# Where the v requests stand in GpSimd's queue: each v behind the k of its unit, two stores held back at the end, half a row slot as first transfer

## The chip, the cores and the metric

One core of one Trainium2 chip. The metric is the device time of the whole kernel in microseconds (us). Every kernel is run several times. "Span" is the time from the first to the last instruction of the one run that was profiled. It lies 1 to 2 us below the device time of that run. An engine "lands" when its part of a transfer has arrived; each transfer is shared by all 16 DMA engines, and the first and the last of them can land some microseconds apart.

## The reference

Local attention in windows of 64 rows, fp32 in and out:

```python
B, S, D, W = 4, 4096, 1536, 64
q_w, k_w, v_w = (x.reshape(B, S // W, W, D) for x in (q, k, v))
logits = np.einsum('bnwd,bnud->bnwu', q_w, k_w) * D ** -0.5
attn = softmax(logits)                       # over u, the 64 keys of the window
out = np.einsum('bnwu,bnud->bnwd', attn, v_w).reshape(B, S, D)
```

Every element of q, k and v is read once and every element of the output is written once: 302 MB and 101 MB.

## The kernel before

The 16384 rows are worked in N = 32 units of 512 rows. A unit has three loads (q, k, v: 3 MB of fp32, which land as 1.5 MB of fp16) and one store (3 MB of fp32). GpSimd issues all of them, except the first load (raw q of unit 0) and the second half of the last store, which SyncE issues. GpSimd also hands each landed tile over to the buffer that TensorE reads: it waits for the landing, copies (2.75 us), and requests the next load into the buffer that is free again. So the order of GpSimd's program is the order of the requests, and all of them stand in one queue, q0.

```python
def load(name, u, dst, s):
    r = R if name == "v" else SLOTS          # v in pieces of 2 rows, q and k of 4
    nc.gpsimd.dma_start(out=slots(dst, 0, SLOTS, r), in_=rows(src, u * UR, SLOTS, r)).then_inc(s, 16)

def hand_over(src, dst, d, u, m, g):         # wait for landing and for a free target, copy, tell TensorE
    gp.wait_ge(d, 16 * u); gp.wait_ge(m, copies[0] // 3 + 1)
    gp.tensor_copy(out=dst[...], in_=src[...]).then_inc(c_l, 1)
    ...
# --- start: raw q of unit 0, three transfers by SyncE; the identity waits for the first of them
for sl, s in ((slice(0, 1), d_r0), (slice(1, 2), d_r1), (slice(2, SLOTS), d_r2)):
    nc.sync.dma_start(out=outs[0][:, sl, :], in_=raw[:, sl, :]).then_inc(s, 16)
...
for u in range(1, NV + 1):                   # NV = 2 buffers for v
    load("v", u, vls[u % NV], d_v[u % NV])
# --- the loop
for u in range(1, N):
    hand_over(ql, q16, d_q, u, m_q, g_q)
    if u + 1 < N: load("q", u + 1, ql, d_q)
    hand_over(kl, k16, d_k, u, m_k, g_k)
    if u + 1 < N: load("k", u + 1, kl, d_k)
    for what in {N - 3: "", N - 2: "-v"}.get(u, "s"):
        if what == "v": load("v", N - 1, vls[(N - 1) % NV], d_v[(N - 1) % NV])
        else:
            gp.wait_ge(m_q, u + 1)
            store(u - 2 if what == "-" else u - 1)
    if u == N - 2: store(u - 1)
    hand_over(vls[u % NV], v16, ...)
    if u + NV < N - 1: load("v", u + NV, vls[u % NV], d_v[u % NV])
# --- the end: two half stores of the last unit, one by GpSimd, one by SyncE; then gp.drain(), waits, clearing
```

The softmax here doesn't subtract the row's maximum and nothing guards it: scores larger than these inputs give would overflow.

## Time and profile before

| what | value | where |
|---|---|---|
| time | 946.71 us, 946.34 to 946.71 | median and range of 3 runs |
| span of the profiled run | 946.4 us (this run took 948.15 us, more than the three above) | page |
| DMA engines busy by q0 | 100.0% of 16 engines | page, queues |
| busiest compute engine | PE, 69% | page, engines |

A copy on GpSimd whose idle time was ended by a DMA marks the landing of its tile on the last of the 16 DMA engines. In a row of GpSimd's timeline stand start, duration, engine, line, operation and tiles, and in brackets the idle time just before with what ended it. The prediction shows the lines and reads them.

### The profile page before, as it was taken

Reading aid. Unit: us, or ns where it says so; the run is one execution under the profiler, and the core shown is the slowest. Engines: PE = TensorE matmul, PEld = TensorE weight load, DVE = VectorE, ACT = ScalarE, POOL = GpSimd, SP = SyncE. Lnnn points to the kernel's source line nnn. Section 1 sums busy time; section 2 is a strip of 40 time slices with the busy share of each in tenths; the row PEclk is TensorE's granted clock in tenths of the full one; section 3 lists DMA queues with packets and bytes.
Section 4 is the critical chain, followed back from the end, with each engine's and each line's share of the span. In section 5 each row is a group of like instructions: output and inputs, shape, how many; then the busy total and the mean of one; then the engine's idle time right before and its main releaser. Section 6 shows DMA issues by size and latency. Waiting matters only on the chain. (4 is left out here: it accounts for less than half of the span.)

```text
span 946.4 us, 11421 instructions
## 1 busy us (share of the span) xinstructions
PE 651.0 (69%) x4096; PEld 419.8 (44%) x3456; DVE 279.7 (30%) x453; ACT 332.8 (35%) x642; POOL 341.5 (36%) x229
## 2 busy tenths in 40 slices
PE   2776866768667676667777667866768666777682
PEld 2544543445534345434554344543435533445450
DVE  1333223332233231333313323223322233232331
ACT  1433323333334342333423334323333234343252
POOL 4323343233442334423344323343233442333520
PEclk9989777897878887798878789878898879797897
DMA  9999999999999999999999999999999999999997
GB/s 250 216 229 270 283 281 282 242 257 283 281 280 258 243 282 282 278 270 236 278 282 280 279 238 265 282 280 282 249 251 283 283 281 264 238 279 283 197 315 321
DMA packets 26940, 253.35 MB, mean 268 GB/s; under 512 B 2096, under 2 KB 2096, under 8 KB 10544
## 3 DMA queue, kind: packets, MB, share of 16 engines
q0 software_dynamic: 26352, 248.52, 100.0%
q1 hardware_dynamic: 576, 4.72, 1.3%
q14 instruction: 10, 0.08, 0.0%
q8 instruction: 2, 0.03, 0.0%
HBM read 301.99 MB, written 100.66 MB: 425 GB/s over the span
## 5 line engine op out<-in xcount | busy, mean ns | idle before, releaser
L147 PE MATMUL tp<-ident,q 128*128 128x128 f32 x768 | 165.0, 384 | 185.6 <-PEq L213 172.7
L147 PEld LDWEIGHTS tp<-ident,q 128*128 128x128 f32 x768 | 131.2, 200 | 239.4 <-issue 236.8
L292 POOL COPY q<-ql 128x3072 f32<-128x3072 f32 x31 | 85.0, 2743 | 395.7 <-DMA ql<-in_q_dram 395.5
L159 PE MATMUL lt<-xq,xk 128*128 128x256 f16 x1536 | 210.2, 288 | 0.0
L147 PE MATMUL tp<-ident,k 128*128 128x128 f32 x768 | 136.3, 317 | 67.3 <-PEq L213 54.5
L159 PEld LDWEIGHTS lt<-xq,xk 128*128 128x128 f16 x1536 | 156.8, 102 | 30.4
L222 ACT COPY xq<-tp 128x512 f32<-128x512 f32 x96 | 60.2, 627 | 291.2 <-ACTq L213 291.2
L147 PEld LDWEIGHTS tp<-ident,k 128*128 128x128 f32 x768 | 105.1, 163 | 86.3 <-issue 83.9
L222 DVE COPY xq<-tp 128x512 f32<-128x512 f32 x96 | 66.4, 692 | 254.7 <-DVEq L213 254.7
L222 ACT COPY xk<-tp 128x512 f32<-128x512 f32 x96 | 59.8, 623 | 228.6 <-ACTq L213 228.6
L222 DVE COPY xk<-tp 128x512 f32<-128x512 f32 x96 | 66.5, 693 | 198.6 <-DVEq L213 198.6
L292 POOL COPY k<-kl 128x3072 f32<-128x3072 f32 x31 | 85.3, 2751 | 110.5 <-DMA kl<-in_k_dram 110.5
L264 ACT ACTIVATE et<-lt,zeros 32x128 f16<-32x128 f32 x256 | 92.0, 359 | 39.4 <-ACTq L213 36.1
L188 PEld LDWEIGHTS <-et 128*128 128x128 f16 x384 | 30.2, 97 | 152.7 <-issue 116.7
L115 PE MATMUL o<-v,et 128*128 128x512 f16 x384 | 93.3, 379 | 0.0
L251 DVE TENSOR_SCALAR out<-o,rs 128x512 f32<-128x512 f32 x128 | 90.2, 747 | 7.7
L292 POOL COPY v<-vl 128x3072 f32<-128x3072 f32 x31 | 85.5, 2758 | 10.4 <-DMA vl<-in_v_dram 10.4
L115 PE MATMUL tp<-v,et 128*128 128x512 f16 x256 | 75.8, 377 | 0.0
L241 DVE RECIPROCAL rs<-sp 128x2 f32<-128x2 f32 x64 | 10.6, 166 | 162.6 <-DVEq L213 162.4
L275 ACT ACTIVATE out<-tp,rs 128x512 f32<-128x512 f32 x64 | 44.0, 688 | 37.2 <-ACTq L213 31.3
L251 DVE TENSOR_SCALAR out<-tp,rs 128x512 f32<-128x512 f32 x64 | 48.1, 751 | 26.2 <-DVEq L213 26.2
L115 PE MATMUL lt<-v,et 128*128 128x512 f16 x128 | 48.3, 377 | 0.0
(22 smaller groups left out, 201.2 us busy)
## 6 DMA issues: line engine op xcount, KB each, us to landing
out_dram<-out POOLq DMA_DIRECT2D x31, 3072.0 KB, 32.5
ql<-in_q_dram POOLq DMA_DIRECT2D x31, 1536.0 KB, 25.8
kl<-in_k_dram POOLq DMA_DIRECT2D x31, 1536.0 KB, 25.8
vl<-in_v_dram POOLq DMA_DIRECT2D x31, 1536.0 KB, 35.7
out<-in_q_dram SPq DMA_DIRECT2D x2, 768.0 KB, 6.5
out<-in_q_dram SPq DMA_DIRECT2D x1, 1536.0 KB, 11.2
k<-in_k_dram POOLq DMA_DIRECT2D x1, 1536.0 KB, 12.2
v<-in_v_dram POOLq DMA_DIRECT2D x1, 1536.0 KB, 18.8
```

The costliest lines, as they stand in the source:

```text
L115: return nc.tensor.add_instruction(mybir.InstMatmult(name=nc.get_next_instruction_name(), engine=PE, ins=[low(rhs), low(w)], outs=[low(o)] ...
L147: ins = nc.tensor.transpose(tps[g % 2][:, r, j, :], pairs[:, c * P : (c + 1) * P], ident[:, :])
L159: ins = nc.tensor.matmul(lts[h][:, r, :, :], lhsT=halves(xk, c)[:, r, h, :, w], rhs=halves(xq, c)[:, :, h, :, w], start=(c == 0 and w == 0 ...
L188: ld = nc.tensor.ldweights(w)
L222: copy(out=dst, in_=tps[g % 2][:, :, :, :]).then_inc(f_c[g % 4], 1)
L241: ve.reciprocal(out=rs[:, n : n + R], in_=sp[:, n : n + R]).then_inc(n_d, 1)
L251: ins = ve.tensor_scalar_mul(scaled(u, n, j), bank(n, j), scalar1=rs[:, n : n + 1])
L264: ins = sc.activation(ets[h][s, :, :, s], lts[h][s, :, :, s], EXP, bias=zeros[s, 0:1], scale=scale)
L275: ins = sc.activation(scaled(u, n, j), bank(n, j), COPY, bias=0.0, scale=rs[:, n : n + 1])
L292: gp.tensor_copy(out=dst[:, :, :].bitcast(FP32), in_=src[:, :, :].bitcast(FP32)).then_inc(c_l, 1)
```

## The change

Its intent: request v(u+1) right behind k(u+1), instead of v(u+2) after the copy of v(u). At the end the last loads are then all queued before the two stores that were held back, so the queue does not run dry between them. At the start the first transfer is half as large, so that the identity, and the first request behind it, come sooner.

```diff
@@ start: the first row slot as two halves
-        for sl, s in ((slice(0, 1), d_r0), (slice(1, 2), d_r1), (slice(2, SLOTS), d_r2)):
-            nc.sync.dma_start(out=outs[0][:, sl, :], in_=raw[:, sl, :]).then_inc(s, 16)
+        for lo, hi, c0, c1, s in (
+            (0, 1, 0, D // 2, d_r0), (0, 1, D // 2, D, d_r1), (1, 2, 0, D, d_r2), (2, SLOTS, 0, D, d_r3)
+        ):
+            nc.sync.dma_start(out=outs[0][:, lo:hi, c0:c1], in_=raw[:, lo:hi, c0:c1]).then_inc(s, 16)
   [...]
         load("k", 1, kl, d_k)
-        for u in range(1, NV + 1):
-            load("v", u, vls[u % NV], d_v[u % NV])
+        load("v", 1, vls[1], d_v[1])
@@ loop
             if u + 1 < N:
                 load("k", u + 1, kl, d_k)
-
-            for what in {N - 3: "", N - 2: "-v"}.get(u, "s"):
-                if what == "v":
-                    load("v", N - 1, vls[(N - 1) % NV], d_v[(N - 1) % NV])
-                else:
-                    gp.wait_ge(m_q, u + 1)
-                    store(u - 2 if what == "-" else u - 1)
-            if u == N - 2:
+                load("v", u + 1, vls[(u + 1) % NV], d_v[(u + 1) % NV])
+
+            if u != N - 3:
+                gp.wait_ge(m_q, u + 1)
+                if u == N - 2:
+                    store(u - 2)
                 store(u - 1)
             hand_over(vls[u % NV], v16, d_v[u % NV], (u + u % NV) // NV, m_v, g_v)
-            if u + NV < N - 1:
-                load("v", u + NV, vls[u % NV], d_v[u % NV])
```

More of the change, by code (lines that the diff above doesn't have):

```diff
@@ L74 @@
     sp = ps("sp", [P, 4])
-    d_r0, d_r1, d_r2, d_q, d_k, d_k0, d_v0 = (
-        sem(n) for n in ("d_r0", "d_r1", "d_r2", "d_q", "d_k", "d_k0", "d_v0")
+    d_r0, d_r1, d_r2, d_r3, d_q, d_k, d_k0, d_v0 = (
+        sem(n) for n in ("d_r0", "d_r1", "d_r2", "d_r3", "d_q", "d_k", "d_k0", "d_v0")
     )
@@ L301 @@
         raw = rows(qf, 0, SLOTS, SLOTS).rearrange("p h (r d) -> p (h r) d", d=D)
-        for sl, s in ((slice(0, 1), d_r0), (slice(1, 2), d_r1), (slice(2, SLOTS), d_r2)):
-            nc.sync.dma_start(out=outs[0][:, sl, :], in_=raw[:, sl, :]).then_inc(s, 16)
+        for lo, hi, c0, c1, s in (
+            (0, 1, 0, D // 2, d_r0), (0, 1, D // 2, D, d_r1), (1, 2, 0, D, d_r2), (2, SLOTS, 0, D, d_r3)
+        ):
+            nc.sync.dma_start(
+                out=outs[0][:, lo:hi, c0:c1], in_=raw[:, lo:hi, c0:c1]
+            ).then_inc(s, 16)
         nc.vector.memset(ident[:, :], 0.0).then_inc(i_d, 1)
@@ L314 @@
         for i in range(SLOTS):
-            nc.gpsimd.wait_ge((d_r0, d_r1, d_r2, d_r2)[i], 16)
+            nc.gpsimd.wait_ge((d_r1, d_r2, d_r3, d_r3)[i], 16)
             nc.gpsimd.tensor_copy(out=q16[:, i, :], in_=outs[0][:, i, :]).then_inc(c_q, 1)
```

## The prediction

> **What bounds the kernel now.** I read the page from the top: engine shares, slices, DMA queues, traffic, the ended chain, then the DMA issues. After that came the stage table, and last GpSimd's own timeline, because GpSimd issues nearly every transfer.
>
> ```profile
> PE 651.0 (69%) x4096; PEld 419.8 (44%) x3456; DVE 279.7 (30%) x453; ACT 332.8 (35%) x642; POOL 341.5 (36%) x229
> ...
> DMA  9999999999999999999999999999999999999997
> GB/s 250 216 229 270 283 281 282 242 257 283 281 280 258 243 282 282 278 270 236 278 282 280 279 238 265 282 280 282 249 251 283 283 281 264 238 279 283 197 315 321
> ...
> q0 software_dynamic: 26352, 248.52, 100.0%
> ...
> HBM read 301.99 MB, written 100.66 MB: 425 GB/s over the span
> ```
>
> No compute engine is above 69%, while the DMA row is at 9 in every slice but the last, and GpSimd's queue q0 alone fills 100% of the 16 engines. So the transfers bound it. The GB/s row counts landed bytes: a load reads fp32 and lands fp16, so it counts half of what it reads. Counted by the larger side, load and store cost alike, and all of it, 402.65 MB, runs at 425 GB/s. The chain of waits is useless here: its pieces cover under 1 us around 929 us, because what ends the span is a store, and the chain does not follow that.
>
> ```profile
> 840.00:856.00 16.00, 8.73 (x60) 3.49 (x39) 4.57 (x8) 7.21 (x15) 2.76 (x2) 0.87 1.05 221
> 868.00:884.00 16.00, 9.62 (x68) 4.22 (x46) 5.26 (x9) 7.21 (x15) 2.20 (x1) 0.96 1.04 219
> 884.00:888.00 4.00, 2.98 (x13) 2.60 (x14) 0.69 (x1) 0.62 (x1) 1.08 (x2) 0.50 0.94 178
> 888.00:892.00 4.00, 2.29 (x13) 1.53 (x11) 1.39 (x2) 1.26 (x2) 2.75 (x1) 0.82 1.06 224
> 892.00:904.00 12.00, 10.53 (x86) 7.64 (x78) 2.65 (x5) 5.28 (x12) 8.15 (x6) 1.00 0.96 188
> ...
> 924.00:932.00 8.00, 5.42 (x32) 0.80 (x9) 4.57 (x8) 3.72 (x6) 0.55 (x1) 1.00 1.02 433
> ```
>
> The last two columns are DMA share and GB/s landed. Loads alone land 219 to 221 (twice that is read), stores alone 433. In two stretches of loads, 884 to 888 and 892 to 904 us, the share falls below 1 and the rate to 178 and 188. These are the only weak stretches between the start and the final drain.
>
> ```profile
> 823.47 2.74 POOL L292 COPY q<-ql 128x3072 f32<-128x3072 f32 x1 [13.16 <-DMA ql<-in_q_dram]
> ...
> 852.64 2.74 POOL L292 COPY q<-ql 128x3072 f32<-128x3072 f32 x1 [13.16 <-DMA ql<-in_q_dram]
> ...
> 863.86 2.76 POOL L292 COPY v<-vl 128x3072 f32<-128x3072 f32 x1
> 881.80 2.75 POOL L292 COPY q<-ql 128x3072 f32<-128x3072 f32 x1 [15.18 <-DMA ql<-in_q_dram]
> 885.13 0.53 POOL L108 DMA_DIRECT2D ql<-in_q_dram  x1 [0.58 <-POOL q L292]
> 889.07 2.75 POOL L292 COPY k<-kl 128x3072 f32<-128x3072 f32 x1 [3.41 <-DMA kl<-in_k_dram]
> 892.41 0.53 POOL L108 DMA_DIRECT2D kl<-in_k_dram  x1 [0.58 <-POOL k L292]
> ...
> 906.36 2.75 POOL L292 COPY k<-kl 128x3072 f32<-128x3072 f32 x1 [5.57 <-DMA kl<-in_k_dram]
> ...
> 929.57 0.55 POOL L382 DMA_DIRECT2D out_dram<-out  x1 [5.89 <-ACT out L275]
> ```
>
> A copy that waits for a landing marks it. Two q copies lie 29.17 us apart: one unit is three loads and a store, so 29.17 / 4 = 7.29 us per transfer. From 889.07 (k of unit 30 landed) to 906.36 (k of unit 31) only two transfers land, yet it takes 17.29 us where 2 x 7.29 = 14.58 are due: 2.7 us lost. The reason is in the issue times. In that iteration the store and the v of the last unit are deferred, so when q of unit 31 is requested at 885.13 only the rest of k 30 is queued (landed by 889.07), and k 31, requested at 892.41, has only q 31 ahead of it. The queue is nearly dry twice.
>
> **What the Trainium skill says.** "DMA: Bandwidth & Descriptors", section "Issuing engines are not separate DMA queues": transfers started by different engines run on the same 16 DMA engines and interleave, so the issuer saves only issue time. The trace agrees: loads and stores add up to one 425 GB/s. The same page, "Specifications", gives a fabric ceiling of 435 GB/s for a core; stores alone reach 433 here, so there is no headroom to find in a reordering, only idle time. The same page, "Anatomy of one DMA — SWDGE (gpsimd) path", puts a fixed cost of about 2 us on a transfer issued from GpSimd. That is hidden while others are queued; the 2.7 us above is where it shows.
>
> **The change part by part.**
>
> 1. v behind k. Before, GpSimd queues q(u+1), k(u+1), store(u-1), v(u+2); after, q(u+1), k(u+1), v(u+1), store(u-1). Same transfers, same sizes, and no instruction is added to any engine in the loop (229 on GpSimd are reordered; SyncE has 11 rows for 10). Per unit the bytes stay, so 29.17 us stay. When q lands there are still k, v and a store behind it, about 22 us of backlog. Gain 0.
>
> 2. The tail. Store 28 and store 29 are held until the v of unit 31 is requested. The requests now run k 30, v 30, q 31, k 31, v 31, store 28, 29, 30, 31. q 31 is requested 3.3 us after q 30 lands (881.80 to 885.13 above), with k 30 and v 30 behind it: 2 x 7.29 - 3.3 = 11 us of backlog. k 31 then has v 30 and q 31 ahead of it, the same 11 us. Neither can run dry, so the 2.7 us return. A second count: before, 12 transfers remain when q 29 lands at 852.6, so 852.6 + 12 x 7.29 = 940.1; the last store landed at 929.57 + 13.3 (page, issues) = 942.9, 2.8 us late. A third: against 220 GB/s the weak stretches lack (42 x 4 + 32 x 12) / 220 = 2.5 us. I take 2.7.
>
> 3. Does compute then become the end? After, q 29 lands one transfer earlier (its v no longer precedes it), at 845.3; k 31 at 845.3 + 8 x 7.29 = 903.6, v 31 at 910.9, stores 28, 29, 30 at 918.2, 925.5, 932.8. From a k copy to the first output was 14.4 us (889.07 to 903.50) and to the end of the last 19.6 us (889.07 to 908.69). Unit 31 writes the buffer that store 28 empties, so 903.6 + 14.4 = 918.0 meets 918.2: it may wait a microsecond, and be done near 924 or 925. The queue has work to 932.8. The last half stores join a busy queue with 8 us to spare, against 5 before (942.9 - 7.3 - 930.6). The end stays the DMA's.
>
> 4. The start. The first transfer is 384 KB instead of 768 KB, so the wait of 6.5 us before the identity, and with it the first k request at 7.51, comes earlier: half of 0.79 MB at 420 GB/s is 0.9 us, and more (1.5) if the cold first microsecond is shared. The engines are fed from 2 us on and in the 8 to 12 us windows their share is 1.01 and 1.06, so I find at most 0.5 us there; I count 0.2. Two extra issues are one more row on SyncE, 0.44 us (1.33 / 3), in parallel.
>
> Sum: 946.7 - 2.7 - 0.2 = 943.8 us.
>
> **The rivals.** (a) A hidden bound: v now lands only 7.3 us after its k, is copied by 10.1 us (with 2.75 us of copy), and the weighted product needs it 12.9 us after the k copy starts (889.07 to 902.00). It has 2.8 us of slack; if late DMA engines eat that, PE waits, but PE already idles 5.8 us per unit ahead of the q transposes (185.6 us on the page over 32 units), so the time stays at 943.8. (b) The start turns bad: the early k shares the engines with the rest of raw q, in packets that are larger, so raw q lands 3 to 5 us later and the first matmul moves from 16.4 to about 20. PE is late by that in unit 0, catches up within two units, and requests are queued deep by then; worth 0. (c) Nothing comes back, because the 2.7 us is lost for another reason, such as a slow DMA engine or GpSimd writing four requests in a row; then 946 to 947. Against it: the same copies and requests happen in every unit with no dip in the rate. (d) Three loads in a row or two stores in a row run slower than an alternation. Stores alone (433) and loads alone (2 x 220) are both at full rate, so no.
>
> **Range and chances.** The mechanism leaves a gain between 1 us (one of the two holes stays) and 4.5 us (tail, start, and a slow DMA engine lagging less). That gives 942.3 to 945.6. 2% is 19 us; nothing in the idle columns is that large, and the work is unchanged: within 2% at 0.985.
>
> **What would show it.** Right: the steady distance of q copies still 29.2 us; k 30 to k 31 with three transfers between (v 30, q 31, k 31) at about 3 x 7.29 = 21.9 us; load stretches near the end at 219 or more; last half stores issued near 925 and landing some 15 us later. Wrong: a new hole after the last loads, GpSimd waiting for v in the loop long enough to delay q requests, a unit longer than 29.3 us, or the last stores issued after 933, which would put compute at the end.

## The result, and the profile after

| | median | range | runs |
|---|---|---|---|
| before | 946.71 us | 946.34 to 947.0 | 4 |
| after | 950.02 us | 948.98 to 952.19 | 4 |

The ratio of after to before is 1.0038, with a 95% interval of 1.0017 to 1.0059. A ratio here is the mean time of one kernel's fast runs over that of the other's of the same rounds, so it is not quite the ratio of the medians. The class, within 2%, came as predicted, but the time did not: 3.3 us slower by the medians where 2.9 us faster was said, and outside the range of 942.3 to 945.6. The run of after that was profiled (948.98 us, span 947.2 us) was its fastest, so its trace shows less of the loss than the median has. The profiled run of before took 948.15 us, 1.4 us more than its median. The two traces therefore stand closer together than the two kernels do.

These are the lines of after's page that answer to those of before.

```profile
DMA  9999999999999999999999999999999999999997
GB/s 252 218 226 267 284 281 276 241 257 282 281 282 248 246 283 282 281 264 238 277 283 281 274 238 267 283 282 277 238 258 283 283 277 250 247 282 283 217 326 304
...
q0 software_dynamic: 26352, 248.52, 100.0%
...
HBM read 301.99 MB, written 100.66 MB: 425 GB/s over the span
```

The page looks as before. The engines count as busy, the same bytes move, and the rate of 425 GB/s is the same to three digits. A loss of 0.4% is not to be seen here, and a DMA engine that works longer on a packet than usual counts as busy all the same.

The table by stage of after, with the stretches of the end; the last two columns are DMA share and GB/s landed.

```profile
868.00:884.00 16.00, 9.01 (x48) 3.88 (x28) 5.54 (x10) 6.00 (x12) 3.30 (x2) 0.79 1.01 217
884.00:888.00 4.00, 1.49 (x12) 1.18 (x11) 1.10 (x2) 1.25 (x2) 2.81 (x2) 0.88 1.06 220
888.00:892.00 4.00, 3.87 (x19) 3.02 (x18) 1.38 (x2) 0.62 (x1) 2.66 (x5) 0.50 1.04 218
892.00:904.00 12.00, 11.25 (x82) 6.76 (x64) 3.03 (x5) 5.99 (x13) 5.42 (x2) 0.92 1.02 216
...
942.00:944.00 2.00, 0.00 (x0) 0.00 (x0) 0.00 (x0) 0.00 (x0) 0.00 (x0) 0.50 0.07 31
```

The two weak stretches of before (178 and 188 GB/s) are gone: all the last loads run at 216 to 220. In the last line, from 942 to 944 us, a share of 0.07 is left, where before has 0.01: a few DMA engines are late. The last four of the 16 landings of GpSimd's half store are at 942.09, 943.07, 943.52 and 943.69 us. In before a single one is late, at 942.87, and the next landed at 940.88.

GpSimd's timeline of after, one unit of the loop and the end.

```profile
818.86 2.75 POOL L292 COPY q<-ql 128x3072 f32<-128x3072 f32 x1 [11.82 <-DMA ql<-in_q_dram]
826.13 2.75 POOL L292 COPY k<-kl 128x3072 f32<-128x3072 f32 x1 [3.39 <-DMA kl<-in_k_dram]
829.48 0.54 POOL L108 DMA_DIRECT2D kl<-in_k_dram  x1 [0.60 <-POOL k L292]
830.01 0.71 POOL L108 DMA_DIRECT2D vl<-in_v_dram  x1
830.70 0.73 POOL L281 DMA_DIRECT2D out_dram<-out  x1
833.60 2.74 POOL L292 COPY v<-vl 128x3072 f32<-128x3072 f32 x1 [2.17 <-DMA vl<-in_v_dram]
848.15 2.75 POOL L292 COPY q<-ql 128x3072 f32<-128x3072 f32 x1 [11.81 <-DMA ql<-in_q_dram]
...
884.61 2.74 POOL L292 COPY k<-kl 128x3072 f32<-128x3072 f32 x1 [3.40 <-DMA kl<-in_k_dram]
...
906.54 2.75 POOL L292 COPY k<-kl 128x3072 f32<-128x3072 f32 x1 [4.53 <-DMA kl<-in_k_dram]
...
926.06 0.54 POOL L383 DMA_DIRECT2D out_dram<-out  x1 [8.98 <-ACT out L275]
```

Four things are to be seen. The q copies are 848.15 - 818.86 = 29.29 us apart, and over 23 units the mean is 29.31 us (before 29.23). Three requests stand back to back from 829.48 to 831.43, and this is while v is landing: its last engine is done at 833.60. Behind that v stands a store, so in these microseconds the engines pass from a load to a store. From k 30 to k 31 it takes 906.54 - 884.61 = 21.93 us, as predicted for three transfers. And the last half stores are requested at 926.06, long before the queue is empty, so compute is not the end.

**Two counts over the trace's packet records.** A transfer is split into packets. In the loop a load packet of q or k takes 926 ns (12288 bytes landed) and one of v 474 ns (6144 bytes); a store packet of 12288 bytes takes 460 ns. I counted between 200 and 840 us the load packets that took over 40 ns more than that, and the store packets that took 465 to 560 ns (leaving out 473 ns, a value that every kernel shows). The excess is given as the time of one engine per unit. The kernels named below before appear in the experiments; in those whose names begin with vq, v is requested right behind q.

```
                     load packets stretched   store packets stretched
                     count  engine-us/unit    count  engine-us/unit
before                  24   0.21               71   0.06
after                  166   1.31              236   0.23
whole_start            278   2.36              260   0.24
store_late              52   0.29              175   0.19
late_from_2              1   0.01              183   0.20
store_behind_q           3   0.01              172   0.21
v_behind_q              25   0.18                0   0.00
vq_control              18   0.14                0   0.00
vq_delayed              34   0.21                1   0.00
vq_delayed_9            87   0.77                5   0.01
```

In after the stretched load packets are nearly all of v (2.55 of the 2.56 us that the mean engine loses this way from 40 to 875 us; before loses 0.39). In the unit above there are 16 of them, and they begin between 828.2 and 831.7 us. Six of these had ended by 829.3, before the first request's record begins at 829.48. Over the loop 41 of after's 166 stretched load packets end before the first request of their unit begins, and 128 of 278 in whole_start. So nearness to the requests is seen, but a request that stretches only what is under way during it does not account for all of these packets.

**Where the span ends.** The two half stores of the last unit land last. I took the mean of their landings over the engines, the lag from there to the very last landing, and what follows until the end of the span.

| kernel | mean landing | lag of the last | to the end of the span | span |
|---|---|---|---|---|
| before | 940.59 | 2.28 (GpSimd's half) | 3.50 | 946.37 |
| after | 939.70 | 3.99 (GpSimd's) | 3.50 | 947.20 |
| before_filled_tail | 937.88 | 3.22 (SyncE's) | 1.34 | 942.44 |
| late_from_2 | 937.70 | 5.75 (GpSimd's) | 3.50 | 946.95 |
| store_behind_q | 938.01 | 5.98 (GpSimd's) | 3.63 | 947.61 |
| v_behind_q | 938.03 | 2.46 (SyncE's) | 1.34 | 941.83 |
| vq_last_k_first | 938.61 | 2.63 (SyncE's) | 3.04 | 944.28 |

So between these two traces after gained 0.9 us on the mean engine, but its last engine is 1.7 us further behind the mean than that of before. (The profiled run of before was a slow one, see above.) The last column but one has its own reason: the drain of GpSimd ends 2.26 us after the landing of GpSimd's own half in 18 of the 20 traces, and 1.2 us of clearing follow. Where GpSimd's half is the last by far, the span ends 3.50 us after it; where SyncE's is, 1.34 us after that one.

### The profile page after: what moved, and what is told of

It is laid out like the page before. It is cut to its first block, busy times and chain, and to the rows that moved or that the text cites. A ratio compares the mean times of both kernels' runs of the same rounds, so it can differ in the third digit from the quotient of the medians.

```text
span 947.2 us, 11422 instructions
## 1 busy us (share of the span) xinstructions
PE 650.3 (69%) x4096; PEld 418.6 (44%) x3456; DVE 279.6 (30%) x453; ACT 332.3 (35%) x642; POOL 340.9 (36%) x229
## 5 line engine op out<-in xcount | busy, mean ns | idle before, releaser
L147 PE MATMUL tp<-ident,q 128*128 128x128 f32 x768 | 162.3, 379 | 190.0 <-PEq L213 175.2
L147 PEld LDWEIGHTS tp<-ident,q 128*128 128x128 f32 x768 | 129.1, 197 | 243.3 <-issue 241.3
L159 PE MATMUL lt<-xq,xk 128*128 128x256 f16 x1536 | 212.4, 290 | 0.0
L292 POOL COPY v<-vl 128x3072 f32<-128x3072 f32 x31 | 85.1, 2744 | 68.1 <-DMA vl<-in_v_dram 68.1
## 6 DMA issues: line engine op xcount, KB each, us to landing
out<-in_q_dram SPq DMA_DIRECT2D x1, 1536.0 KB, 13.3
out_dram<-out POOLq DMA_DIRECT2D x1, 1536.0 KB, 17.6
```

The source lines that it names most:

```text
L147: ins = nc.tensor.transpose(tps[g % 2][:, r, j, :], pairs[:, c * P : (c + 1) * P], ident[:, :])
L159: ins = nc.tensor.matmul(lts[h][:, r, :, :], lhsT=halves(xk, c)[:, r, h, :, w], rhs=halves(xq, c)[:, :, h, :, w], start=(c == 0 and w == 0 ...
L292: gp.tensor_copy(out=dst[:, :, :].bitcast(FP32), in_=src[:, :, :].bitcast(FP32)).then_inc(c_l, 1)
```

## The experiments

The theory after the result, here called the request theory: the requests k, v and store of one unit, in one run on GpSimd, fall into the microseconds in which the engines pass from v to a store, and this stretches the packets under way; the loop gets longer and eats the gain of the tail. The rivals: the new start costs it; the tail gains nothing; the landing of v just behind k makes GpSimd wait, which delays requests; or the order of the transfers itself, three loads in a row, is slow, whenever they are requested. Runs stand beside runs of before on the same chip: its medians were 947.12, 947.09, 947.05, 947.04 and 947.32 us in the five calls.

### First call

**half_start_only**: before with the new start alone.

The main line of the diff, cut:

```diff
+ (0, 1, 0, D // 2, d_r0), (0, 1, D // 2, D, d_r1), (1, 2, 0, D, d_r2), (2, SLOTS, 0, D, d_r3)
```

> The kernel before with only the half row slot first. Theory S (the start made the result worse: the early k and the last rows of raw q share the engines, one engine begins late and stays late): about 948 to 949 us, later engines' lag visible in k landings from the first unit on. Theory T (each unit loses time where the v load gives way to the store while requests are made): the start is worth nothing or up to 0.5 us, so 946.2 to 947.0 us.

Measured: 946.54 us (945.75 to 946.97), ratio 0.9993 (0.998 to 1.0006). The start does no harm, so the rival of the start falls. Its predicted gain of 0.2 us is inside what these runs cannot resolve.

**whole_start**: after with the start of before, so the rest of the change alone (the diff above, reversed).

> The changed kernel with the start of the kernel before. Theory S: the loss goes, 943.5 to 945 us. Theory T: the loss stays, 949 to 951 us, and single runs differ by 2 to 3 us as they do for the changed kernel.

Measured: 951.16 us (949.37 to 952.27), ratio 1.0038 (1.0025 to 1.0051). The loss does not sit in the start. It is the kernel with the most stretched load packets of all, 2.36 engine-us per unit, and its units take 29.41 us.

**late_requests**: after, but GpSimd hands v over before it requests k, v and store, which puts these three requests about 7 us later, behind the pass from v to the store.

```diff
             hand_over(kl, k16, d_k, u, m_k, g_k)
+            late = u < N - 3
+            if late:
+                hand_over(vls[u % NV], v16, d_v[u % NV], (u + u % NV) // NV, m_v, g_v)
             if u + 1 < N:
                 load("k", u + 1, kl, d_k)
   [...]
-            hand_over(vls[u % NV], v16, ...)
+            if not late: hand_over(vls[u % NV], v16, ...)
```

> The changed kernel, but in all units up to the last three the requests for k, v and the store are made after the copy of v, some 7 us later, when the engines are already in the store; the order of transfers in the queue is unchanged. Theory T1 (GpSimd writing three requests while v is loaded stalls the load): the stall goes, q copies 29.17 us apart, 944 to 945.5 us. Theory T2 (the switch of the engines from v load to store costs, whoever is issuing): nothing changes, 949 to 951 us and the v packets are still stretched.

Measured: 950.34 us (949.8 to 950.85), ratio 1.0032 (1.0019 to 1.0045). No gain, but the run does not speak against the request theory: the stretched load packets between 200 and 840 us are gone altogether (none), and the edit made a hole of its own near 54 us, where k of unit 2 was requested too late (1.25 us of the mean engine).

**before_filled_tail**: before with only its tail changed, so that v of the last unit is requested one iteration earlier and the stores are held as in after.

```diff
-            for what in {N - 3: "", N - 2: "-v"}.get(u, "s"): ...
+            if u != N - 3:
+                gp.wait_ge(m_q, u + 1)
+                if u == N - 2: store(u - 2)
+                store(u - 1)
             hand_over(vls[u % NV], v16, ...)
-            if u + NV < N - 1:
+            if u + NV < N:
                 load("v", u + NV, vls[u % NV], d_v[u % NV])
```

> The kernel before with its own order in the loop and its own start, only the tail filled: the v of the last unit is requested at its regular place at the end of iteration 29, and stores 28 and 29 are held until k 31 is requested. If the prediction's hole is real: the 2.7 us come back without the loop's loss, 943.5 to 944.5 us, and from the k copy of unit 30 to that of unit 31 three transfers pass in 21.9 us. If the hole was only idle time of the fast engines while the slow one sets the end: 945.5 to 946.7 us.

Measured: 944.22 us (943.91 to 945.71), ratio 0.9972 (0.996 to 0.9985), which is 0.0028 x 947.1 = 2.65 us less. The tail is worth what was predicted, so the rival of the tail falls. GpSimd's timeline of this kernel at the end shows it.

```profile
888.66 2.74 POOL L292 COPY k<-kl 128x3072 f32<-128x3072 f32 x1 [3.40 <-DMA kl<-in_k_dram]
...
910.97 2.75 POOL L292 COPY k<-kl 128x3072 f32<-128x3072 f32 x1 [4.99 <-DMA kl<-in_k_dram]
```

From k 30 to k 31 three transfers land in 22.3 us, where 3 x 7.29 = 21.9 are due; before it was two in 17.3. The mean landing of the last half stores moved from 940.59 to 937.88, by 2.71 us (before's trace is of a slow run, so that this agrees so well with 2.7 is in part luck). What filled the hole is only in part an empty queue: between 876 and 925 us before has 58 stretched packets of q and k, 1.66 us of the mean engine, and before_filled_tail has none.

### Second call

**late_from_4**: late_requests, but only from unit 4 on (`late = 4 <= u < N - 3`), where the queue is deep.

> The late requests again, only from unit 4 on, so that the queue is filled at the start as in the changed kernel: the run before lost its gain in one hole near 54 us that its own edit made (k of unit 2 asked for too late), while no v packet was stretched after it. Theory T1 (three requests written by GpSimd while the engines pass from load to store stall the load): 943.3 to 945 us, 5 us under the changed kernel. Theory T2 (the order q, k, v, store costs in itself): 948 us or more.

Measured: 948.76 us (948.52 to 949.24), ratio 1.0016 (1.0003 to 1.003). The stretched load packets are gone in the loop (one left). The time hardly follows: it is 1.3 us below after's median of 950.02, but only 0.4 below that of after_again (949.14), and the intervals of the ratios overlap (1.0003 to 1.003, against 1.0017 to 1.0059 and 1.0015 to 1.0046). Most of the loss stays: 1.5 us above before, and 4.5 above before_filled_tail, which has the same tail. So the request theory as I had stated it is not the whole.

**v_behind_q**: after, with v requested right behind q instead of right behind k. The same transfers, the same tail, but the run of requests k, v, store is broken up into q, v and k, store.

```diff
                 load("q", u + 1, ql, d_q)
+                load("v", u + 1, vls[(u + 1) % NV], d_v[(u + 1) % NV])
             hand_over(kl, k16, d_k, u, m_k, g_k)
             if u + 1 < N:
                 load("k", u + 1, kl, d_k)
-                load("v", u + 1, vls[(u + 1) % NV], d_v[(u + 1) % NV])
   [...]                                         # at the start, too, v of unit 1 moves ahead of its k
```

> The changed kernel with v requested right behind q, so the queue is q, v, k, store: q and v are requested during loads, k and the store are requested while a store is under way, and nothing is requested at the switch from load to store. T1: no stretched packets at the switch, 943.3 to 945 us. T2 in the form that any three loads in a row followed by a store cost: 948 us or more.

Measured: 943.6 us (943.38 to 944.48), ratio 0.9964 (0.9951 to 0.9978). It beats both kernels: before by 3.5 us and after by 6.4 (950.02 - 943.6; the two come from different calls, and against after_again it is 5.5). The gain over before is the gain of the tail and the start: filled_half has before's order of v and the ratio 0.9965. So v behind q costs nothing, and v behind k does. Here, too, three loads stand in a row between two stores, so the rival that three loads in a row are slow in themselves falls. In its timeline the requests are these.

```profile
816.29 2.75 POOL L292 COPY q<-ql 128x3072 f32<-128x3072 f32 x1 [7.21 <-DMA ql<-in_q_dram]
819.62 0.56 POOL L108 DMA_DIRECT2D ql<-in_q_dram  x1 [0.58 <-POOL q L292]
820.18 0.71 POOL L108 DMA_DIRECT2D vl<-in_v_dram  x1
830.89 2.75 POOL L292 COPY k<-kl 128x3072 f32<-128x3072 f32 x1 [10.01 <-DMA kl<-in_k_dram]
```

q has landed on the last engine at 816.29 and k lands at 830.89, so at 819.6 to 820.9 the engines are in the v between them, a load behind a load and before a load. k and the store are requested after 830.89, when the pass from k to the store is over. No request falls into a pass from load to store, and no store packet is stretched.

**filled_half**: before_filled_tail with the new start.

> The kernel before with the filled tail and the half row slot at the start: if both gains of the prediction are real and independent (2.9 us and 0.6 us by the two single runs), 943.3 to 944.3 us.

Measured: 944.21 us (943.22 to 944.64), ratio 0.9965 (0.9952 to 0.9979), against 944.22 without it. What the change meant to gain is to be had, and the start adds nothing that can be measured.

**v_whole_rows**: after, with v loaded in pieces of four rows like q and k. The result is wrong (relative error 1.38), because the pieces no longer lie where the product looks for them.

```diff
-        r = R if name == "v" else SLOTS
+        r = SLOTS
```

> Wrong result on purpose: the changed kernel with v loaded four rows to a partition, so its packets land 12288 bytes like those of q and k and not 6144. If the stall hangs on v's small packets: it goes, 943.5 to 945.5 us. If it hangs on requests at the switch: it stays, 948.5 to 951 us.

Measured: 948.23 us (947.31 to 949.99), ratio 1.0015 (1.0001 to 1.0029). Larger v packets lose a little less (1.80 us of the mean engine against 2.56 in after), but the effect stays, and so do the stretched store packets (185 of them). The small packets of v are not its cause.

### Third call

**late_from_2**: late_requests from unit 2 on (`late = 2 <= u < N - 3`), to see whether two more units change anything.

> Late requests from unit 2 on. The run from unit 4 on had no stretched packet after 200 us, but its first units had them and left the last of the 16 engines some 2 us further behind than it was at the start, and the end waits for that engine. If requests at the switch are the whole cause: no stretched packets in units 2 to 6 either, last engine 2 us earlier, 945 to 946.5 us. If the switch from v to store stretches packets in early units without any request: 948 to 949.5 us again.

Measured: 948.87 us (948.72 to 949.04), ratio 1.0016 (1.0003 to 1.003), as from unit 4 on. The three requests now stand behind the copy of v.

```profile
832.50 2.75 POOL L292 COPY v<-vl 128x3072 f32<-128x3072 f32 x1 [4.56 <-DMA vl<-in_v_dram]
835.85 0.54 POOL L108 DMA_DIRECT2D kl<-in_k_dram  x1 [0.60 <-POOL v L292]
836.38 0.71 POOL L108 DMA_DIRECT2D vl<-in_v_dram  x1
```

One stretched load packet is left in the loop. Its mean engine lands at 937.70, as early as that of v_behind_q (938.03), and still the span is 5.1 us longer. By the table above, all of it lies on the last engine (3.3 us) and in the drain behind it (2.2 us). From k of unit 5 to k of unit 28 the mean engine lost 0.34 us against 23 undisturbed units (29.167 us each, 670.84), and the last 2.71 us; in v_behind_q it was 0.32 and 0.44. So there is a second effect: one engine falls behind, about 0.1 us per unit, and does not catch up. At the end it lands at 943.45, and the next of the 16 at 940.13. The stretched store packets fit to it: they follow each other without a gap, as packets of one engine do (starts 424.70, 425.18, 425.67, 426.15 in one unit), and they add up to 0.20 us per unit.

**store_late**: k and v requested as in after, only the store after the copy of v.

```diff
                 load("v", u + 1, vls[(u + 1) % NV], d_v[(u + 1) % NV])
+            if late: hand_over(vls[u % NV], v16, ...)       # late = 2 <= u < N - 3
             if u != N - 3:
                 ...
                 store(u - 1)
-            hand_over(vls[u % NV], v16, ...)
+            if not late: hand_over(vls[u % NV], v16, ...)
```

> Dose: k and v are requested at the switch as in the changed kernel, only the store's request moves behind the v copy (from unit 2 on). If each request at the switch adds stalls: about two thirds of the changed kernel's stretched packets, 947.5 to 949.5 us. If only the store's request matters: as the late run, 945 to 946.5 us.

Measured: 949.25 us (948.39 to 950.51), ratio 1.0023 (1.0009 to 1.0037). The stretched load packets fall from 1.31 to 0.29 engine-us per unit though k and v stay where they were, and the time stays that of after_again (949.14). So it is the run of three, or the store in it, that goes with most of the stretching; k and v alone go with a little. The late engine is there as before.

**vq_delayed**: v_behind_q, with seven spare copies by GpSimd (6.2 us in all) ahead of the requests of q and v, to move these two towards the pass from k to the store.

```diff
             hand_over(ql, q16, d_q, u, m_q, g_q)
+            if 2 <= u < N - 3:
+                for _ in range(7):
+                    gp.tensor_copy(out=spare[:, 1, :], in_=spare[:, 0, :]).then_inc(c_s, 1)
+                    gp.wait_ge(c_s, ...)
             if u + 1 < N:
                 load("q", u + 1, ql, d_q)
                 load("v", u + 1, vls[(u + 1) % NV], d_v[(u + 1) % NV])
```

> The kernel with v behind q (943.6 us), but GpSimd spends some 7 us on copies in a spare buffer before it requests q and v, so the two requests fall at the switch from the k load to the store. Requests at a switch from load to store are the cause: stretched k packets appear, over 1 us of them on the mean engine, and 945 to 948 us. The cause lies in v next to the store: 943.3 to 944.3 us.

Measured: 944.98 us (944.21 to 945.71), ratio 0.9977 (0.9963 to 0.9991).

**vq_control**: the same seven copies behind the two requests, so that GpSimd does the same work and nothing is requested later.

> Control: the same seven copies of GpSimd, but after the requests of q and v. Both theories: no change against v behind q, 943.3 to 944.3 us, under 0.6 us of stretched packets.

Measured: 943.46 us (942.96 to 944.23), ratio 0.9959 (0.9946 to 0.9973). The copies cost nothing; the later requests cost 1.5 us. The shift was too short to tell much.

### Fourth call

**vq_delayed_9** and **vq_delayed_11**: vq_delayed with nine and eleven copies instead of seven.

> v behind q, with the requests of q and v held back by nine copies of GpSimd, some 1.8 us later than with seven: that run asked 3.1 to 1.8 us before the first engine passed to the store, a little early, and gave 945.0 us against 943.5 of its control. If requests at the switch are the cause: more stretched k packets than with seven (0.45 us on the mean engine), 945 to 947 us. Otherwise: 943.3 to 945 us and no more of them.

> The same with eleven copies, the requests another 1.8 us later, inside the switch. If requests at the switch are the cause: as many stretched packets as with nine or more, 945 to 948 us. Otherwise: 943.3 to 945 us.

Measured: nine copies 947.1 us (946.49 to 947.63), ratio 1.0001 (0.9988 to 1.0014); eleven copies 947.24 us (946.24 to 947.52), ratio 1.0001 (0.9989 to 1.0014). Against vq_control this is 3.6 and 3.8 us more, for nothing but two requests that come later while the queue stays full. First GpSimd's timeline of vq_delayed_9, one unit.

```profile
324.57 7.94 POOL L372 COPY spare<-spare 128x768 f32<-128x768 f32 x9 [0.17 <-POOL q L294]
332.81 0.56 POOL L110 DMA_DIRECT2D ql<-in_q_dram  x1 [0.30 <-POOL spare L372]
333.37 0.71 POOL L110 DMA_DIRECT2D vl<-in_v_dram  x1
336.49 2.75 POOL L294 COPY k<-kl 128x3072 f32<-128x3072 f32 x1 [2.41 <-DMA kl<-in_k_dram]
```

Then that of vq_control.

```profile
323.22 0.56 POOL L110 DMA_DIRECT2D ql<-in_q_dram  x1 [0.59 <-POOL q L294]
323.78 0.71 POOL L110 DMA_DIRECT2D vl<-in_v_dram  x1
324.48 6.19 POOL L375 COPY spare<-spare 128x768 f32<-128x768 f32 x7
334.56 2.75 POOL L294 COPY k<-kl 128x3072 f32<-128x3072 f32 x1 [3.89 <-issue]
```

With nine copies the requests end 2.4 us before k is landed on the last engine, so they stand in the pass from k to the store; in the control they end some 10 us before its copy. The mean engine loses 1.25 us to stretched packets from 40 to 875 us (control 0.25), and from unit 5 to 28 the last engine loses 3.55 us (control 0.25). So the effect is made in a kernel that did not have it. Two rivals bear on it. The queue is shallower when q is requested (an estimate from the landings: some 11 us of transfers are left), but late_from_2 requests k with as little left and has one stretched load packet. And the spare copies were moved with the requests: on the median they end 2.1 us after the first engine has landed k, and in the control 1.2 us before it. Of the 87 stretched packets 42 overlap a spare copy and 29 end before the request of q begins; with eleven copies it is 43 and 32 of 52. The copies were not moved alone, so these runs do not separate them from the requests.

**store_behind_q**: after, with the store requested right behind q, which takes it out of the run of three.

```diff
                 load("q", u + 1, ql, d_q)
+            if 2 <= u <= N - 3:
+                gp.wait_ge(m_q, u)
+                store(u - 2)
             hand_over(kl, k16, d_k, u, m_k, g_k)
   [...]
-            if u != N - 3:                       # the store behind k and v, now only at the end
+            if u >= N - 2:
```

> The changed kernel with one thing moved: in the loop the store is requested behind the next q, so the queue is k, v, q, store; k and v are still requested together right behind each other, but v no longer stands next to the store and nothing is requested while the engines pass from load to store. If the place of the v requests at the switch is the cause: 943.3 to 945 us, few stretched v packets. If v right behind k costs in itself: 948 us or more.

Measured: 949.39 us (949.18 to 949.55), ratio 1.0027 (1.0014 to 1.004). The stretched load packets are gone (0.01 engine-us per unit), and the time does not fall. The mean engine is early (938.01), but its last engine ends 5.98 us after that (943.98 us, the next at 939.58). The store packets are still stretched, as in all kernels with v right behind k (0.21 engine-us per unit), which fits to one late engine. It is the second effect alone, and of the two branches above it is the second: v right behind k costs in itself.

**after_again**: after, unchanged, on the chip of this call.

> The changed kernel itself beside the other runs of this call, for its scatter: 949 to 951.5 us, several us between single runs.

Measured: 949.14 us (948.63 to 952.49, 6 runs), ratio 1.0031 (1.0015 to 1.0046). The slowdown repeats, and so does what the trace shows: 0.83 engine-us per unit in load packets, 0.21 in store packets.

### Fifth call

**vq_last_k_first**: v_behind_q, but v of the last unit requested behind its k, so that TensorE gets the last k earlier. It was meant to be a still better version.

```diff
-                load("v", u + 1, ...)                    # behind q
+                if u + 1 < N - 1: load("v", u + 1, ...)
   [...]
                 load("k", u + 1, kl, d_k)
+                if u + 1 == N - 1: load("v", u + 1, ...)
```

> v behind q in the loop, but for the last unit k is requested ahead of v. In v behind q the last k is the last load, unit 31 ends only at 930.7 us, and the DMA share in 924 to 932 us falls to 0.90: compute is the end there. If that is so, the share is 1.0 again and 0.8 to 1.5 us come back: 942.2 to 943.0 us, the best version. If the last engine sets the end anyway: 943.2 to 943.8 us.

Measured: 946.52 us (945.88 to 946.69), ratio 0.9994 (0.9979 to 1.0009). A miss, and some 3 us slower than v_behind_q. Its timeline shows a part of why.

```profile
877.04 0.53 POOL L108 DMA_DIRECT2D ql<-in_q_dram  x1 [0.58 <-POOL q L292]
888.31 2.75 POOL L292 COPY k<-kl 128x3072 f32<-128x3072 f32 x1 [10.74 <-DMA kl<-in_k_dram]
891.64 0.53 POOL L108 DMA_DIRECT2D kl<-in_k_dram  x1 [0.58 <-POOL k L292]
892.16 0.71 POOL L108 DMA_DIRECT2D vl<-in_v_dram  x1
892.86 1.43 POOL L281 DMA_DIRECT2D out_dram<-out  x2
```

I had taken away what stood in the queue: when k of the last unit is requested at 891.64, only its q is ahead of it, and that q has landed on the first engine at 893.03. It looks like the shallow queue of before's tail again, though here, too, GpSimd makes four requests meanwhile. Ten packets of q or k are stretched from 892.9 to 894.3 us, by up to 1.28 us (0.32 us of the mean engine); in before it was 58 of them and 1.66 us in its two weak stretches, and in v_behind_q none. But the larger part I cannot lay to that: 42 packets of the last v are stretched from 905.7 to 909.3 us (1.30 us of the mean engine), where that v passes into the two stores. GpSimd requests nothing in these microseconds, and the queue holds two stores. In after's tail the same v stands ahead of the same two stores, and only 2 packets are stretched. So a request close by is not the only thing that can stretch a v ahead of a store. On the mean engine most of the loss comes back by the end (938.61 against 938.03), but GpSimd's half now lands at 940.77 on its last engine instead of 937.11, and with its drain and clearing it ends the span 2.5 us later.

**vq_whole_start**: vq_last_k_first with the start of before.

> The same with the start of the kernel before. If the half row slot is worth its predicted 0.2 to 0.6 us: that much slower than the run above. If it is worth nothing, or costs a late engine: the same within 0.3 us or faster.

Measured: 947.03 us (946.74 to 947.36), ratio 1.0 (0.9985 to 1.0015). It repeats the miss, with 38 stretched v packets at the same place. In this pair the half slot is worth 0.5 us; in the pairs above it was 0.6 and 0.0. Each is within the spread of the runs, so the start is worth between 0 and 0.6 us, and I cannot say more.

## Why the prediction was wrong, point by point

1. **"v behind k ... Per unit the bytes stay, so 29.17 us stay ... Gain 0." This is the step that failed.** The bytes stayed and the queue stayed deep, as said. But the time of a unit is not set by bytes and depth alone; it also depends on the order and the moment of GpSimd's requests. The units took 29.31 us in after's fastest run, against 29.23 in before, 29.19 in v_behind_q and 29.18 in vq_control. The tail gave -2.65 us and the result was +3.3 us, so the term that I set to 0 was worth about +6 us at the medians (3.3 + 2.65); v_behind_q, with the same bytes and the same tail, is 5.5 to 6.4 us faster than after. Two effects were found. Load packets are stretched around the requests that fall into a pass from load to store: moving the requests away (late_from_2) brought the mean landing from 939.70 to 937.70, and moving requests, with copies, into the pass (vq_delayed_9 against vq_control) cost 3.6 us. And with v right behind k one engine falls behind, with stretched store packets beside it, which leaves the end to it: store_behind_q shows this alone, 949.39 against 943.6 for v_behind_q, with the same mean landing. How the 6 us divide between the two is not shown, for in late_from_2 the last engine still landed at 943.45, against 943.69 in after. My own test for this step, "a unit longer than 29.3 us", is what the trace showed.

2. **The tail, 2.7 us: right in size, and its reason in part.** before_filled_tail gained 2.65 us, and after's own tail shows the loads without a gap. But of the 2.7 us 1.66 us of the mean engine were packets that took longer, not engines without work; that a deeper queue took these away was not foreseen. Nor were the two stretches the only ones with a share below 1: in steps of 4 us it was 0.95 at 848 to 852 us. What I had not seen is that the end hangs on which half store lands last, because GpSimd's drain takes another 2.26 us behind its own.

3. **Compute does not become the end: right.** I said that the last stores would be requested near 924 or 925 and land some 15 us later; it was 926.06 and 17.6 us, and k 31 was there at 906.5 instead of 903.6.

4. **The start, 0.2 us: not resolved**, as told at the runs. The step itself failed: the first transfer was half as large, but the first k request came at 7.37 instead of 7.51 us, 0.14 us earlier and not 0.9. Rival (b) came in part: the first matmul moved from 16.37 to 19.00 us and the last part of raw q landed 13.3 instead of 11.2 us after its request, without any cost at the end.

5. **Rival (a), GpSimd waiting for v: the wait came, and was harmless.** It is 68.1 us in all on after's page (31 x 2.2), and PE's idle time ahead of the q transposes grew only from 185.6 to 190.0 us. v_behind_q removes it, but vq_delayed_9 has no such wait and is slow all the same.

6. **Rival (c) was answered with "the same copies and requests happen in every unit with no dip in the rate".** The argument was true of before's loop, and I carried it over to after, where the requests stand elsewhere. In before's tail the rival came in part: of the 1.66 us about 0.8 begin from 894 to 898 us, behind four requests in a row (892.41 to 895.06). But before_filled_tail makes three at that place with more in the queue, and nothing is stretched. **Rival (d)** I dismissed from the rates of pure loads and pure stores. Those rates were right, but the stretched load packets sit between them, in the pass from one to the other, which a mean over a stretch of either does not contain.

**What stays open.** That the stretched load packets go when the requests are moved is shown (late_from_2), and that they come when requests and copies are moved into the pass (vq_delayed_9). Why packets take longer then is not, nor why many of them end before the first request begins, and the tail of vq_last_k_first, where v packets are stretched with no request near, says that the requests act on something that can also come about without them. The Trainium skill, "DMA: Bandwidth & Descriptors", section "SWDGE vs HWDGE vs iDMA", says that GpSimd appends the descriptors of its transfers to rings in SBUF and that the engines drain these packet by packet. A clash between GpSimd's writing and the engines' reading there would fit, but no run here separates it from others. Open, too, is why some store packets, one engine's by their times, are about 5% longer (484 ns on average in late_from_2, for 460) in every kernel with v right behind k (172 to 260 of them in the table), less often with a store between k and v (71 in before), and hardly ever with v behind q (at most 5). Moving the requests (late_from_2) or the store (store_behind_q) did not change it. That the drain costs 2.2 us where GpSimd's half store is last is read from the traces and was not tried by itself.

## What to carry to other kernels

When the DMA engines bound a kernel, an order of requests is not free because its bytes are the same: look at what the engines are doing at the moment of each request, and try other orders, and the runs of requests away from the pass between loads and stores. Here v behind q instead of v behind k was 5.5 to 6.4 us better at the same bytes. And when such a kernel ends, ask for the last of the 16 engines and not for the mean; an engine that lags through the loop ends it, and whatever drain stands behind the queue it belongs to comes on top.

## What the Trainium skill lacked or had wrong

- "DMA: Bandwidth & Descriptors", section "Anatomy of one DMA — SWDGE (gpsimd) path", says of descriptor generation: "You can emit a lot of descriptors before the incremental cost shows up". The section has nothing on when they are emitted. In these runs two requests of 0.56 and 0.71 us, moved by some 8 us (from 3.3 to 11.2 us after the start of the q copy) into the pass from a load to a store, together with the spare copies ahead of them, cost 3.6 us over the kernel (943.46 to 947.1), and stretched packets took 1.25 us of the mean engine instead of 0.25.
- The same page, section "Latency and other measured facts", says that two of the DMA engines are usually slower than the others in traces, with a cause that it calls not certain. The records here carry no engine number, but they agree that an engine is late, and add that it depends on the order of the requests: over 23 units the last engine lost 2.98 us with v behind k (store_behind_q) and 0.44 us with v behind q, while the mean engine lost 0.37 and 0.32.
- No page that I read says what a drain on GpSimd costs behind its own last transfer: it ended 2.26 us after that landing in 18 of 20 traces (1.77 and 2.38 in the others).
- The page's statement in "Issuing engines are not separate DMA queues", that only issue time is saved by another issuer, agrees with the bandwidth here (421 GB/s in after_again from 932 to 938 us, with a half store of each issuer in the queues, and 433 for GpSimd's stores alone in before from 924 to 928 us). Nearly all other transfers are GpSimd's, so the 425 GB/s that the prediction names is no test of it. But the half store that SyncE requested ended the span 1.34 us after its landing, and GpSimd's 3.50 us.
